# Both in-projections of a hybrid decoder layer as one list of slots, issued in program order

## The chip, the cores and the metric

The kernel runs on one core of one Trainium2 chip. The metric is the device time of one execution in microseconds (us), as the median of several runs. The core has a matrix engine (PE, with weight loads shown as PEld), a vector engine (DVE), a scalar engine (ACT), GpSimd (POOL) and a queue engine (SP). Each takes its instructions from a stream of its own, in order. DMA transfers are issued by SP, ACT and POOL, and are also taken from each of these queues in order. A DMA whose data is not ready, or whose destination is not free, holds everything that stands behind it in the same queue.

## The reference

One layer with 2048 tokens, width 1024, all in float32. A combined input projection makes 19 tiles of 128 channels, three token mixers work on them, an output projection merges them, and a squared-ReLU MLP follows.

```python
h = rmsnorm(x, norm1_g)
z = jnp.einsum("bsd,dc->bsc", h, w_in)
y_attn = attention_mixer(q, k, v)          # 6 heads, windows 128/512/2048, dilations 1/4/16
y_conv = conv_module(a, gate, ...)         # a * sigmoid(gate), causal conv of 31 taps, LayerNorm, silu
y_lru  = recurrent_mixer(gate, xr, ...)    # gelu(gate) * RG-LRU(causal conv of 4 taps)
x = x + jnp.einsum("bsc,cd->bsd", jnp.concatenate([y_attn, y_conv, y_lru], -1), w_out)
h2 = rmsnorm(x, norm2_g)
x = x + jnp.einsum("bsf,fd->bsd", jnp.square(jax.nn.relu(jnp.einsum("bsd,df->bsf", h2, w_up))), w_down)
return rmsnorm(x, final_g)
```

## The kernel before

Tokens are worked in two halves of 1024 (h = 0 and 1). Every float32 matrix is split into a rounded part and a rest, and each product is three matmuls: high by high, high by low, low by high. The split of a tile is a cast on ACT and a subtraction on DVE (`split`; `halves` does the same behind the in-projection).

The in-projection of a half makes 16 channel tiles (q and k tiles 0 to 5, conv tiles 9 to 12, recurrent tiles 13 to 18) and, apart from them, the value columns (tile -1, "V"). `COLUMN_ORDER` sets the order of the tiles; the first three of half 0 and the last two of each half are worked side by side, the others one by one. A tile takes eight steps k over the input channels. I call one step of one tile a **slot**: six matmuls of 512 columns (V: twelve of 384). There are 288 slots, 144 a half. `project` runs the steps, `load_w` loads and splits the weights of four steps, `Acts.more` loads and splits x (eight chunks of 128 channels, two loads each) and adds its squares. The sum of squares, by `norm`, becomes the factor r1 with which `evac` (and `project_v`) scales a finished tile out of PSUM on DVE. The scaled tile goes to DRAM by SP; gate tiles pass a sigmoid or gelu on ACT first. There are four main PSUM banks (two tiles), three "mix" banks and one "conv" bank.

While PE works on slots, `tick` issues pieces of half 0's mixers: attention (`attention`), then the recurrent mixer (`lru_mixer`) and the merge of the attention heads (`combine`), and as a filler the convolution on DVE (`conv_whole`, with `conv_norm` for its LayerNorm, then `conv_ahead` for half 1). In the recurrent mixer of half 0 both gates use the one conv bank: three matmuls, a sigmoid on ACT, and then three matmuls of the other gate. Half 1's mixers run later, beside the output projection and the MLP.

`out_first` loads the first operands of the output projection, `out_split` and `act_split` split them. The rows named `pair`, and `rounded` numbers 79 to 83 around the end of the in-projection, are these operands; `rounded_83` also holds the in-projection's weights.

The order of each engine's stream is made by a scheduler from priorities (`first()` and `low()` raise and lower them) and from edges written by hand: `chain` and `step` keep a mixer's instruction behind the last main instruction issued before it, and `issue_after` ties a DMA or a split to an earlier instruction. Where no edge holds, an instruction may stand elsewhere than the program wrote it.

Of the kernel before, what the change touches and what calls it, by code (L numbers as in the profile page):

```python
# [9 lines left out]
OP = mybir.AluOpType  # L10
PSUM = bass.MemoryType.PSUM

P = 128
# [66 lines left out]
def body(tc, xt, w_in, w_v, w_out, w_up, w_down, vecs, lru_wa, lru_wx, consts, g_row, out, out_rows):  # L80
# [222 lines left out]
    def project(src, group, acts, nk, evac, hook=None):  # L303
        banks = [[main_bank() if i < 2 else mix_bank() for _ in range(2)] for i in range(len(group))]
        w = {}
        if not len(acts):
            acts.between = lambda: w.update({0: load_w(src(group[0], 0))})
        for k in range(nk):
            while len(acts) < k + 1:
                acts.more()  # L310
            if hook is not None and k == hook[0]:
                hook[1]()
            for i, t in enumerate(group):
                if k % 4 == 0 and (k or i not in w):
                    w[i] = load_w(src(t, k // 4))
                products(banks[i], w[i], k % 4, acts[k], k == 0, k == nk - 1)
                tick(IN_SHARE)
            while len(acts) < (min(k + 2, nk) if k < 4 else nk):
                acts.more()
        for i, t in enumerate(group):  # L320
            evac(t, banks[i])

    last_x = [None]

    ready = set()

    def inproj(h, after):
        sq = row_tile()

        class Acts(list):  # L330
            between = None

            def more(self):
                k = len(self)
                hh, ll = slot(), slot()
                for blk in range(2):
                    cols = slice(blk * NB, (blk + 1) * NB)
                    raw = raw_tile()
                    dma = nc.sync.dma_start(raw, xt[k][:, h * HS + blk * NB:h * HS + (blk + 1) * NB])
                    if h == 0:  # L340
                        last_x[0] = dma
                    split(raw, hh[:, cols], ll[:, cols], v("norm1_g", k))
                    with tc.high_priority(offset=-20 if h == 0 and k == 0 else 0):
                        sum_squares(sq, k, blk, raw)
                    if self.between is not None:
                        self.between()
                        self.between = None
                self.append((hh, ll))

        acts = Acts()  # L350
        if h:
            while len(acts) < KT:
                acts.more()
        cols_ = groups(COLUMN_ORDER[h], h == 0, True)
        r1 = row_tile()

        def norm():
            for blk in range(2):
                cols = slice(blk * NB, (blk + 1) * NB)
                pair = [X((8 if h else 16) + i)[:, cols] for i in range(2)]  # L360
                split(sq[:, cols], *pair)
                bank = main_bank() if h else (mix_bank, conv_bank)[blk]()
                quarter_mean(bank, pair)
                nc.scalar.activation(r1[:, cols], bank, AF.Sqrt, bias=eps_r, scale=MEAN)
                nc.vector.reciprocal(r1[:, cols], r1[:, cols])

        gates = {}
        held = []
        tok = slice(h * HS, (h + 1) * HS)
        ptok = slice(32 + h * HS, 32 + (h + 1) * HS)  # L370

        def evac(t, banks):
            z = z_tile()
            ready.add((h, t))
            for b, bank in enumerate(banks):
# [3 lines left out]
                if t < CA_T:  # L379
# [10 lines left out]
                    with first():  # L390
                        if t < K_T:
                            nc.vector.scalar_tensor_tensor(zc, src, HD ** -0.5, r, op0=OP.mult, op1=OP.mult)
                        else:
                            nc.vector.tensor_mul(zc, src, r)
                else:
                    with first():
                        nc.vector.tensor_mul(zc, bank, r)
                    if CA_T <= t < CG_T:
                        nc.vector.tensor_mul(zc, zc, gates[t - CA_T][:, cols])
            if t < CA_T:  # L400
                nc.sync.dma_start(zscr[t][:, tok], z)
            elif t < CG_T:
                nc.sync.dma_start(uscr[t - CA_T][:, ptok], z)
# [9 lines left out]
        def project_v():  # L413
            if h == 0:
                nc.sync.dma_start(ident, consts[:, 6 * 256:])
            nc.sync.dma_start(rscr[tok].rearrange("(a n) -> a n", a=1), r1[0:1, :])
            rows = raw_tile()[0:8, 0:P]
            nc.sync.dma_start(rows, rscr[tok].rearrange("(c p) -> c p", p=P))
            bank = (main_bank if h else conv_bank)()
            nc.tensor.transpose(bank[:, 0:HS // P], rows, ident[0:8, 0:8])  # L420
            nc.scalar.copy(rcol[h], bank[:, :HS // P])
            for c0 in range(0, HS // P, 4):
                banks = [main_bank()[:, :VW] for _ in range(4)]
                for k in range(KT):
                    wh, wl = load_w(w_v[k])
                    ah, al = acts[k]
                    for i, bank in enumerate(banks):
# [1329 lines left out]
```

## Time and profile before

| | us |
|---|---|
| median of 3 runs | 2020.29 (2017.7 to 2020.93) |
| the profiled execution, its time | 2015.58 |
| its span, first to last instruction | 2013.4 |
| first in-projection matmul | 7.1 |
| first matmul of the output projection | 537.2 |
| PE busy in the whole span | 1947.4 (97%) |
| mean granted clock of PE | 0.989 |

A profile row of a group gives busy time, the mean of one in ns, and then the idle time that the engine had just before these instructions, with what ended it. The time around the span is 2015.58 - 2013.4 = 2.2 us. In the windows view every engine has its busy time in the stretch, with the number of instructions behind it; PEclk is the share of the full clock that PE was granted.

### The profile page before, as it was taken

How to read it: one execution, taken by the hardware profiler on the slowest of the kernel's cores; microseconds unless marked ns; L12 is line 12 of the kernel's file. 1: busy time of each engine (PE TensorE's matmuls, PEld its weight loads, DVE VectorE, ACT ScalarE, POOL GpSimd, SP SyncE). 2: the span in 40 equal slices, each digit the busy share in tenths (PEclk: the TensorE clock that was granted, in tenths of full speed). 3: DMA queues.
4: the chain of work that ended last, by engine and by line, in shares of the span. 5: the costliest groups of instructions: out<-in, count | busy, mean ns of one | idle time of the engine just before them, and what ended most of it. 6: DMA issues, size and time to landing. Idle time of an engine off the chain costs nothing.

```text
span 2013.4 us, 25522 instructions
## 1 busy us (share of the span) xinstructions
PE 1947.4 (97%) x8906; PEld 1594.7 (79%) x8906; DVE 1448.1 (72%) x1976; ACT 1046.6 (52%) x1631; POOL 203.6 (10%) x360
## 2 busy tenths in 40 slices
PE   7999987997999999999999999999999999999998
PEld 5887766786787777888888887788888888888887
DVE  7886886865477765788868899867555555576884
ACT  6145652434466765456656656546455455444353
POOL 0034200004022423000000000100000000000001
PEclk9999988999999999999999999999999999999999
DMA  5455446357556657544887687764444436786773
GB/s 170 150 175 162 132 133 210 125 196 243 184 185 188 201 149 234 190 146 157 277 278 281 234 290 251 243 199 151 148 150 154 157 141 243 249 285 217 261 262 140
DMA packets 197419, 399.77 MB, mean 199 GB/s; under 512 B 22502, under 2 KB 31094, under 8 KB 197228
## 3 DMA queue, kind: packets, MB, share of 16 engines
q1 hardware_dynamic: 173220, 328.47, 47.7%
q0 software_dynamic: 20624, 58.93, 9.7%
q10 hardware_dynamic: 3448, 10.76, 1.6%
q8 instruction: 70, 1.15, 0.2%
q14 instruction: 57, 0.47, 0.1%
HBM read 287.47 MB, written 119.00 MB: 202 GB/s over the span
## 4 chain that ended last, share of the span: by engine, by line
PE 78%; DVE 7%; DMA 6%; ACT 4%; issue 3%; POOL 1%; SPq 0%; DVEq 0%; ACTq 0%; POOLq 0%
PE bank L1169 9%; PE bank L1168 9%; PE bank L1170 9%; PE bank L1532 8%; PE bank L1531 8%; PE bank L1530 8%; PE mm L268 4%; PE mm L262 4%; PE mm L265 4%; PE bank L981 2%; PE bank L982 2%; PE bank L983 2%; DMA raw<-in_xt 2%; DVE rounded L941 1%; PE mb L726 1%
## 5 line engine op out<-in xcount | busy, mean ns | idle before, releaser
L1168 PE MATMUL bank<-rounded,pair 128*128 128x512 f32 x896 | 351.1, 392 | 1.6 <-ACT low L1177 0.9
L1169 PE MATMUL bank<-rounded,pair 128*128 128x512 f32 x896 | 351.0, 392 | 0.0
L1170 PE MATMUL bank<-rounded,pair 128*128 128x512 f32 x896 | 350.8, 391 | 0.0
L1532 PE MATMUL bank<-rounded,rounded 128*128 128x512 f32 x688 | 268.0, 389 | 1.5 <-DVE rounded L941 1.5
L1530 PE MATMUL bank<-rounded,rounded 128*128 128x512 f32 x688 | 267.8, 389 | 0.0
L1531 PE MATMUL bank<-rounded,rounded 128*128 128x512 f32 x688 | 267.7, 389 | 0.0
L941 DVE TENSOR_TENSOR rounded<-rounded 128x1024 fp32r<-128x1024 f32 (+1 forms) x172 | 186.3, 1097 | 72.6 <-ACT rounded L940 70.1
L940 ACT CAST rounded<-rounded 128x1024 fp32r<-128x1024 f32 (+1 forms) x172 | 160.5, 948 | 142.9 <-DMA rounded<-fscr 104.3
L1168 PEld LDWEIGHTS bank<-rounded,pair 128*128 128x128 f32 x896 | 168.4, 188 | 38.6 <-ACT low L1177 1.4
L1170 PEld LDWEIGHTS bank<-rounded,pair 128*128 128x128 f32 x896 | 168.2, 188 | 35.9 <-issue 0.2
L262 PE MATMUL mm<-rounded,rounded 128*128 128x512 f32 x496 | 163.3, 407 | 34.4 <-ACT rounded L242 21.7
L1169 PEld LDWEIGHTS bank<-rounded,pair 128*128 128x128 f32 x896 | 168.3, 188 | 35.4 <-issue 0.2
L265 PE MATMUL mm<-rounded,rounded 128*128 128x512 f32 x496 | 162.5, 403 | 0.0
L268 PE MATMUL mm<-rounded,rounded 128*128 128x512 f32 x496 | 159.6, 402 | 2.0 <-DVE rounded L243 2.0
L1532 PEld LDWEIGHTS bank<-rounded,rounded 128*128 128x128 f32 x688 | 129.1, 188 | 29.0 <-DVE rounded L941 2.3
L1530 PEld LDWEIGHTS bank<-rounded,rounded 128*128 128x128 f32 x688 | 129.2, 188 | 27.2 <-DVE u L1540 0.2
L1531 PEld LDWEIGHTS bank<-rounded,rounded 128*128 128x128 f32 x688 | 129.1, 188 | 26.9
L940 ACT CAST rounded<-kept 128x1024 fp32r<-128x1024 f32 x80 | 84.1, 1051 | 123.4 <-DVE kept L1340 56.7
L262 PEld LDWEIGHTS mm<-rounded,rounded 128*128 128x128 f32 x496 | 94.4, 195 | 56.4 <-ACT rounded L242 25.0
L242 ACT CAST rounded<-raw 128x512 fp32r<-128x512 f32 (+1 forms) x96 | 54.9, 582 | 143.7 <-PE mm L265 86.0
L940 ACT CAST pair<-wraw 128x1024 fp32r<-128x1024 f32 x64 | 67.1, 1048 | 113.5 <-PE bank L1169 109.3
L941 DVE TENSOR_TENSOR pair<-wraw,pair 128x1024 fp32r<-128x1024 f32 x64 | 78.2, 1222 | 61.5 <-ACT pair L940 61.5
(370 smaller groups left out, 3709.7 us busy)
## 6 DMA issues: line engine op xcount, KB each, us to landing
fscr<-low SPq DMA_DIRECT2D x224, 256.0 KB, 2.2
rounded<-fscr SPq DMA_DIRECT2D x112, 512.0 KB, 3.8
second<-in_w_down SPq DMA_DIRECT2D x80, 512.0 KB, 5.4
kept<-in_w_down SPq DMA_DIRECT2D x48, 512.0 KB, 4.9
raw<-in_w_in SPq DMA_DIRECT2D x64, 256.0 KB, 3.6
low<-in_w_up SPq DMA_DIRECT2D x64, 256.0 KB, 3.2
wraw<-in_w_up SPq DMA_DIRECT2D x64, 256.0 KB, 3.0
raw<-in_xt SPq DMA_DIRECT2D x32, 256.0 KB, 3.8
```

What stands on the lines that cost most here:

```text
L242: nc.scalar.copy(h, raw)
L262: nc.tensor.matmul(bank, wh[:, sl], ah[:, cols], start=first_, stop=False)
L265: nc.tensor.matmul(bank, wh[:, sl], al[:, cols], start=False, stop=False)
L268: nc.tensor.matmul(bank, wl[:, sl], ah[:, cols], start=False, stop=last_)
L940: nc.scalar.copy(h, raw)
L941: nc.vector.tensor_sub(l, raw, f32(h))
L1168: nc.tensor.matmul(bank, wh[:, sl], hi(x), start=fresh and k == 0, stop=False, **kw)
L1169: nc.tensor.matmul(bank, wh[:, sl], lo(x), start=False, stop=False, **kw)
L1170: nc.tensor.matmul(bank, wl[:, sl], hi(x), start=False, stop=k == KH - 1, **kw)
L1530: nc.tensor.matmul(banks[j], th[:, c], sh[:, x], start=fresh and k0, stop=False, **kw)
L1531: nc.tensor.matmul(banks[j], th[:, c], sl[:, x], start=False, stop=False, **kw)
L1532: nc.tensor.matmul(banks[j], tl[:, c], sh[:, x], start=False, stop=k1, **kw)
```

## The change

`inproj`, `project` and `norm` go. `in_projections` writes both halves as one list of 288 slots. For each slot it is fixed at which earlier slot a weight unit is split (four slots ahead of its use, two for V) and at which slot its load is issued (that many plus two slots earlier again), with at most five loads outstanding. The sixteen loads of x for half 1, which stood together, are spread from 40 slots before the turn (slot 144, where half 1 begins) to five slots behind it. x of half 0 is loaded in whole 1024-token chunks into other buffers and split one chunk per three slots. The two norms are generators (`means`) that advance by one piece a slot. `evac` stands right behind a tile's last slot. The DMAs of the norm's row move from SP to POOL, and so does the load of `ident`.

The whole is issued inside `manual_schedule` for all five engines, and the hand-made edges are left out there (`in_order`). The splits of the output projection's first operands (`out_ready`) are issued behind the last slot, and the loads of these operands eight slots before the end of the list instead of sixteen. The matmuls ahead of the output projection are the same in number.

```diff
+    def in_projections(hooks):
+        slots, units, begin = [], [], []
+        for h in range(2):
+            begin.append(len(slots))
+            for grp in groups(COLUMN_ORDER[h], h == 0, True):
+                for c0 in (0, 4) if grp[0] < 0 else (0,):
+                    now = {}
+                    for k in range(KT):
+                        for t in grp:
+                            if t < 0 or k % 4 == 0:
...
+                                units.append(dict(src=src, first=len(slots), lead=2 if t < 0 else 7 if len(slots) == 3 * KT else 4))
+                                now[t] = units[-1]
+                            now[t]["last"] = len(slots)
+                            slots.append((h, grp, c0, k, t, now[t]))
+        turn = begin[1]
+        todo, at = [], 0
+        for n, u in enumerate(units):
+            at = max(at, u["first"] - u["lead"], units[n - 4]["last"] + 1 if n >= 4 else 0)
...
+            todo.append([at, len(todo), at - u["lead"] - 2, load, consume])
...
+        for k in range(KT):
+            for blk in range(2):
+                i = 2 * k + blk
+                at = turn + (4 * i - 40 if k < 4 else 2 * i - 24 if k < 6 else (0, 2, 3, 5)[i - 12])
...
+                todo.append([at, len(todo), at - 6, load, consume])
+        todo.sort(key=lambda x: x[:2])
+        loaded = []
+
+        def pump(s, most=5):
+            while todo and len(loaded) < most and todo[0][2] <= s:
+                x = todo.pop(0)
+                loaded.append((x[0], x[4], x[3]()))
...
+        def means(h):
...
+            for blk in range(2):
+                cols = slice(blk * NB, (blk + 1) * NB)
+                bank = mix_bank()
+                quarter_mean(bank, pairs[blk])
                 nc.scalar.activation(r1[:, cols], bank, AF.Sqrt, bias=eps_r, scale=MEAN)
+            yield
+            for blk in range(2):
+                cols = slice(blk * NB, (blk + 1) * NB)
                 nc.vector.reciprocal(r1[:, cols], r1[:, cols])
+                yield
...
+        norms = {15 + begin[0]: means(0), 7 + turn: means(1)}
+        norm, banks, late = None, {}, []
+        for s, (h, grp, c0, k, t, unit) in enumerate(slots):
+            norm = norms.get(s, norm)
+            if norm is not None:
+                next(norm, None)
+            if s < 14 and (s == 0 or s % 2):
+                x_whole((s + 1) // 2)
+            while loaded and loaded[0][0] <= s:
+                consume_next()
+                pump(s)
+            pump(s)
+            hooks(s, begin, len(slots), h, grp, k, t)
...
+            elif k == KT - 1 and h and s < turn + KT:
+                late.append((h, t, banks[t]))
+            elif k == KT - 1 and t == grp[-1]:
+                for i in grp:
+                    evac(h, i, banks[i])
+            if late and s == turn + 12:
+                evac(*late.pop())
+            tick(IN_SHARE * (1.5 if t < 0 else 1.0))
...
-            if i.engine in held_engines and i.engine in mains:
+            if i.engine in held_engines and i.engine in mains and not in_order[0]:
...
-        last_act = next(i for i in reversed(nc.cur_bb.bb.instructions) if i.engine == mybir.EngineType.Activation)
-        with tc.issue_after(last_act):
-            out_split(0, pairs)
-            for n in range(KT):
-                act_split(1, n)
+
+    def out_ready(pairs):
+        out_split(0, pairs)
+        for n in range(KT):
+            act_split(1, n)
...
-    inproj(1, between)
+    engines = mybir.EngineType
+    in_order[0] = True
+    with tc.manual_schedule(engines={engines.PE, engines.DVE, engines.Activation, engines.SP, engines.Pool}):
+        in_projections(hooks)
+        out_ready(pairs)
+    in_order[0] = False
```

What it does to the streams is seen at three places. The first is SP's queue at the turn between the halves. `raw<-in_xt` are the loads of x for half 1, `raw<-in_w_in` the weight loads. Before:

```order
L339 DMA raw_101<-in_xt 128x512
L339 DMA raw_102<-in_xt 128x512
L339 DMA raw_103<-in_xt 128x512
L339 DMA raw_99<-in_xt 128x512
L411 DMA lscr<-z 128x1024
L251 DMA raw_100<-in_w_in 128x512
L409 DMA gscr<-z 128x1024
L251 DMA raw_101<-in_w_in 128x512
L251 DMA raw_102<-in_w_in 128x512
```

The same place now:

```order
L371 DMA raw_99<-in_xt 128x512
L331 DMA raw_100<-in_w_in 128x512
L371 DMA raw_101<-in_xt 128x512
L371 DMA raw_102<-in_xt 128x512
L371 DMA raw_103<-in_xt 128x512
L331 DMA raw_99<-in_w_in 128x512
L462 DMA lscr<-z 128x1024
L460 DMA gscr<-z 128x1024
L371 DMA raw_100<-in_xt 128x512
L331 DMA raw_101<-in_w_in 128x512
```

The loads of x and of weights now alternate, and the weights of half 1 no longer stand behind all of its x.

The second place is PE in the recurrent mixer: `cb<-mr` are its two gates in the one conv bank, the `mm` rows are slots. Before:

```order
L268 MATMUL mm<-rounded_78,rounded_83 128x512 x2
L576 MATMUL cb<-mr 128x512
L577 MATMUL cb<-mr 128x512
L578 MATMUL cb<-mr 128x512
L576 MATMUL cb<-mr 128x512
L577 MATMUL cb<-mr 128x512
L578 MATMUL cb<-mr 128x512
L262 MATMUL mm<-rounded_81,rounded_83 128x512 x2
L265 MATMUL mm<-rounded_81,rounded_83 128x512
L576 MATMUL cb<-mr 128x512
L577 MATMUL cb<-mr 128x512
L578 MATMUL cb<-mr 128x512
```

And now:

```order
L268 MATMUL mm<-rounded_82,rounded_83 128x512 x2
L634 MATMUL cb<-mr 128x512
L635 MATMUL cb<-mr 128x512
L636 MATMUL cb<-mr 128x512
L634 MATMUL cb<-mr 128x512
L635 MATMUL cb<-mr 128x512
L636 MATMUL cb<-mr 128x512
L262 MATMUL mm<-rounded_82,rounded_83 128x512 x2
L265 MATMUL mm<-rounded_82,rounded_83 128x512 x2
```

Before, most second gates stood some matmuls of a slot behind the first; now all six pairs stand together, and the last pair comes ahead of V, where before three of the twelve triples stood within V.

The third place is ACT at the end of the in-projection. `raw` casts are weights, `z<-z` the gelu of the last tile, `pair` and `rounded_79` to `rounded_83` the operands of the output projection. Its first matmul takes `rounded_79` and `pair_3855` before the change, `rounded_79` and `pair_3891` after it. Before:

```order
L242 CAST rounded_83<-raw_103 128x512
L408 ACT_TABLE_LOAD
L408 ACTIVATE z<-z 128x1024
L940 CAST pair_3855<-pair_3856 128x1024
L940 CAST rounded_79<-rounded_79 128x512 x4
L940 CAST rounded_80<-rounded_80 128x512 x4
L940 CAST rounded_81<-rounded_81 128x512 x4
L940 CAST rounded_82<-rounded_82 128x512
L940 CAST rounded_83<-rounded_83 128x1024
L940 CAST rounded_82<-rounded_82 128x512 x3
L408 ACTIVATE z<-z 128x1024
```

And now:

```order
L242 CAST rounded_83<-raw_100 128x512
L998 CAST rounded_81<-rounded_81 128x512 x2
L998 CAST pair_3893<-pair_3894 128x1024
L998 CAST rounded_83<-rounded_83 128x1024
L998 CAST rounded_81<-rounded_81 128x512 x2
L998 CAST rounded_82<-rounded_82 128x512 x2
L459 ACTIVATE z<-z 128x1024
L998 CAST pair_3891<-pair_3892 128x1024
L998 CAST rounded_79<-rounded_79 128x512 x4
L998 CAST rounded_80<-rounded_80 128x512 x4
```

The casts that the first output matmul needs stood ahead of the last gelu and now stand behind it, and operands that are needed later (`rounded_81`, `rounded_82`, part of `rounded_83`) stand ahead of them.

More of the change, by code (lines that the diff above doesn't have):

```diff
@@ L301, in groups @@
         return out_
[L303 to L321, printed above, removed]
@@ L345, in more @@
[L345 to L357, printed above, removed]
+                    sum_squares(sq, k, blk, raw)
+                todo.append([at, len(todo), at - 6, load, consume])
+        todo.sort(key=lambda x: x[:2])
@@ L358, in norm, with consume_next @@
+        loaded = []
[3 more added lines that the diff above has]
+                loaded.append((x[0], x[4], x[3]()))
+        def consume_next():
+            at, do, raw = loaded.pop(0)
+            do(raw)
+        def means(h):
+            pairs = []
             for blk in range(2):
                 cols = slice(blk * NB, (blk + 1) * NB)
-                pair = [X((8 if h else 16) + i)[:, cols] for i in range(2)]
@@ L361, in norm @@
-                split(sq[:, cols], *pair)
-                bank = main_bank() if h else (mix_bank, conv_bank)[blk]()
-                quarter_mean(bank, pair)
+                pairs.append([X((8 if h else 16) + i)[:, cols] for i in range(2)])
+                split(sq[:, cols], *pairs[-1])
+            for _ in range(3):
+                yield
[3 more added lines that the diff above has]
+                quarter_mean(bank, pairs[blk])
@@ L367, in inproj, with evac @@
+            for _ in range(6):
+                yield
+            bank = mix_bank()
+            nc.tensor.transpose(bank[:, 0:HS // P], rows, ident[0:8, 0:8])
+            nc.scalar.copy(rcol[h], bank[:, :HS // P])
+            yield
         gates = {}
[L368 to L372, printed above, removed]
+        def evac(h, t, banks):
+            ready.add((h, t))
             z = z_tile()
-            ready.add((h, t))
+            tok = slice(h * HS, (h + 1) * HS)
+            ptok = slice(32 + h * HS, 32 + (h + 1) * HS)
@@ L389, in evac @@
                         r = r.rearrange("p (s r) -> p s r", r=16)
[L390 to L394, printed above, removed]
-                else:
[L396 to L399, printed above, removed]
+                    if t < K_T:
+                        nc.vector.scalar_tensor_tensor(zc, src, HD ** -0.5, r, op0=OP.mult, op1=OP.mult)
+                    else:
+                        nc.vector.tensor_mul(zc, src, r)
+                else:
+                    nc.vector.tensor_mul(zc, bank, r)
             if t < CA_T:
```

156 lines of the change are left out of this document (85 added, 71 removed).

## The prediction

> **What bounds the kernel now.** I read the page's first part first: PE is busy for 97% of the span, so a change can only win back PE's idle time and its time at a low clock. Then I cut the in-projection, which ends with the first output matmul at 537.2 us, into stretches (the windows view; the first column after the length is PE's busy time, then PEld, DVE, ACT, POOL, PEclk, DMA share, GB/s):
>
> ```profile
> span 2013.4 us, 25522 instructions
> PE 1947.4 (97%) x8906; PEld 1594.7 (79%) x8906; DVE 1448.1 (72%) x1976; ACT 1046.6 (52%) x1631; POOL 203.6 (10%) x360
> ...
> 7.10:46.80 39.70, 36.50 (x148) 28.55 (x148) 34.07 (x60) 28.11 (x47) 0.00 (x0) 1.00 0.60 184
> 46.80:114.90 68.10, 67.19 (x337) 60.16 (x338) 59.40 (x75) 15.30 (x27) 7.19 (x12) 1.00 0.48 155
> 114.90:225.20 110.30, 108.69 (x610) 84.63 (x609) 77.40 (x182) 61.62 (x165) 43.69 (x72) 1.00 0.57 162
> 225.20:268.20 43.00, 37.14 (x181) 29.52 (x179) 41.58 (x67) 29.47 (x61) 3.06 (x5) 0.99 0.49 153
> 268.20:310.30 42.10, 39.87 (x154) 31.69 (x155) 30.95 (x38) 19.43 (x27) 1.62 (x3) 0.89 0.40 135
> 310.30:332.90 22.60, 11.80 (x52) 9.22 (x50) 12.41 (x14) 6.34 (x7) 0.85 (x2) 0.83 0.23 78
> 332.90:387.00 54.10, 51.07 (x205) 40.74 (x206) 42.74 (x45) 18.88 (x25) 3.47 (x7) 0.91 0.48 170
> 387.00:449.80 62.80, 60.46 (x258) 48.63 (x256) 45.03 (x50) 24.97 (x30) 5.33 (x10) 0.97 0.58 197
> 449.80:500.10 50.30, 37.30 (x202) 34.66 (x202) 27.04 (x50) 20.88 (x32) 17.74 (x33) 0.96 0.73 241
> 500.10:537.20 37.10, 35.85 (x145) 29.03 (x145) 20.05 (x31) 14.86 (x24) 7.75 (x14) 0.92 0.60 186
> ```
>
> PE's idle time is length less busy time; what the clock takes is length times (1 - PEclk). **A**, 7.1 to 225.2 (the first half's tiles up to the end of attention, slots 0 to 119): 3.2 + 0.9 + 1.6 = 5.7 us idle. **B**, 225.2 to 310.3 (around the turn, slots 120 to 167): 5.9 + 2.2 = 8.1 idle and 0.4 + 4.6 = 5.0 of clock. **C**, 310.3 to 537.2: 10.8 + 3.0 + 2.3 + 13.0 + 1.2 = 30.3 idle and 3.8 + 4.9 + 1.9 + 2.0 + 3.0 = 15.6 of clock. That is some 65 us on the table; the matmuls ahead of 537.2 stay the same, and so does the work behind. Who ended PE's waits says the waits view (total, times, longest):
>
> ```profile
> PE mm L262 <- ACT rounded L242: 21.7, 3, 9.3
> PE mm L262 <- DVE z L438: 7.6, 1, 7.6
> ...
> PE cb L576 <- ACT wide L579: 1.8, 2, 1.0
> ```
>
> Weights that were split late (L242), three times for 21.7 us, are just what fixed places address.
>
> **A, worth +2.** Fixed places can take 4 of the 5.7 us. But both row means now take a mix bank while the third tile holds two of three, so the second waits for a square root on ACT with its table load: 1.28 + 0.69 us by the rows below (L518), some 2 us. Sum +2, between -2 (the `setup` splits now wait in order for their loads) and +4.
>
> **B, worth 0.** Here I count DVE's instructions between slots 120 and 168 in the new order. Durations:
>
> ```profile
> L246 DVE SCALAR_TENSOR_TENSOR rounded<-raw,vec,rounded 128x512 fp32r<-128x512 f32 x32 | 23.8, 746 | 3.8 <-ACT rounded L245 3.8
> L277 DVE TENSOR_TENSOR row<-row,tmp 128x512 f32<-128x512 f32 x28 | 19.1, 684 | 0.0
> L397 DVE TENSOR_TENSOR z<-mm,row 128x512 f32<-128x512 f32 x38 | 24.3, 681 | 39.1 <-PE mm L268 38.8
> L365 DVE RECIPROCAL row<-row 128x512 f32<-128x512 f32 x4 | 13.1, 3309 | 1.4 <-ACT row L364 1.4
> L519 DVE RECIPROCAL wide<-wide 128x512 f32<-128x512 f32 x2 | 6.7, 3352 | 2.2 <-ACT wide L518 2.2
> ...
> 342.07 1.28 DVE L486 SCALAR_TENSOR_TENSOR wide<-wide,vec 128x1024 f32<-128x1024 f32 x1
> 343.27 0.69 DVE L243 TENSOR_TENSOR rounded<-raw,rounded 128x512 fp32r<-128x512 f32 x1
> ```
>
> The last two rows show that a tap of 1.28 us lets the next instruction start after 1.20, so I take 0.08 off each. 20 taps x 1.20 = 24.0; 18 splits x 0.61 = 11.0; 11 splits of x at 0.67 and 11 sums at 0.60 = 14.0; 12 evacuations and 12 small operations of the LayerNorm at 0.60 = 14.4; four reciprocals, 13.0; a gate product and the end of attention, 2. Sum 78.4 us, against 85.1 - 8.1 - 5.0 = 72.0 of PE. DVE is the bound there before and after (41.58 of 43.00 us busy in the row 225.20). Five of the sixteen splits of x move ahead of it, but in order DVE stands while ACT does the root ahead of each pair of reciprocals (2.2 and 1.4 us in the rows) and the casts of DVE's own sums: some 7 us, which makes 85. Worth 0; from +12 (PE sets the pace) to -5 (twice the waits).
>
> **C, worth +25.** Of 46 us some waits come back. First the gates of the recurrent mixer (six pairs, one bank). Rows of two such neighbours:
>
> ```profile
> 323.69 1.28 ACT L518 ACT_TABLE_LOAD   x1 [11.01 <-PE cb L283]
> 324.99 0.69 ACT L518 ACTIVATE wide<-cb,eps_l 128x512 f32<-128x512 f32 x1
> ...
> 361.28 0.40 PE L578 MATMUL cb<-mr 128*128 128x512 f32 x1
> 361.72 0.69 ACT L579 ACTIVATE wide<-cb,vec 128x512 f32<-128x512 f32 x1 [15.03 <-PE cb L578]
> 362.46 0.50 PE L576 MATMUL cb<-mr 128*128 128x512 f32 x1 [0.78 <-ACT wide L579]
> ```
>
> Each pair stops PE for 0.8 to 1.0 us (the last row, and the longest of L576 in the waits view), and the first pair of each of three tiles for a table load of 1.28 more, since that load starts only when PE is done: 6 x 0.9 + 3 x 1.28 = 9. [...]
>
> Second, DVE in order behind ACT's exponentials and roots:
>
> ```profile
> L581 DVE TENSOR_TENSOR wide<-wide 128x1024 f32<-128x1024 f32 x3 | 3.6, 1215 | 2.9 <-ACT wide L579 2.9
> L592 DVE TENSOR_TENSOR wide<-wide 128x1024 f32<-128x1024 f32 x3 | 3.7, 1219 | 0.8 <-ACT wide L590 0.8
> L585 ACT ACT_TABLE_LOAD x3 | 3.8, 1283 | 0.1
> L590 ACT ACT_TABLE_LOAD x3 | 3.8, 1283 | 0.1
> L585 ACT ACTIVATE wide<-wide,splus 128x1024 f32<-128x1024 f32 x3 | 3.5, 1153 | 0.0
> L588 ACT ACTIVATE wide<-wide 128x1024 f32<-128x1024 f32 x3 | 3.2, 1056 | 1.3 <-DVE wide L581 1.3
> L590 ACT ACTIVATE wide<-wide 128x1024 f32<-128x1024 f32 x3 | 3.2, 1061 | 1.4 <-DVE wide L589 1.4
> ```
>
> At least 2.9 + 0.8 = 4 us as now; at most the whole ACT chain of three tiles, 3.8 + 3.8 + 3.5 twice (exponential, tanh) + 3.2 + 3.2 = 21. I take 8, nearer the low end, since two to four slots (a slot is six matmuls at 0.227, 1.36 us) lie between the pieces and weights are split four slots ahead. Third, V runs beside the merge of the heads, where DMA moved 241 GB/s (row 449.80) and the longest wait of that stretch (7.6) arose; loads now have a fixed lead of four slots, the output operands no longer stand among them, and I leave 4 us, from 0 to 10. 46 - 9 - 8 - 4 = 25, from 6 (9 + 21 + 10 stay) to 37 (5 + 4 stay, no load late).
>
> **D, the handover, worth -9.** Before, the casts for the output projection ran under the last tile, and PE waited 1.25 us:
>
> ```profile
> 528.65 1.05 ACT L940 CAST rounded<-rounded 128x1024 fp32r<-128x1024 f32 x1 [1.46 <-DMA rounded<-out_w]
> 530.64 1.66 ACT L940 CAST rounded<-rounded 128x512 fp32r<-128x512 f32 x3 [0.93 <-DMA rounded<-mscr]
> 537.05 1.06 ACT L408 ACTIVATE z<-z 128x1024 f32<-128x1024 f32 x1 [4.75 <-DVE z L397]
> 537.16 0.47 PE L981 MATMUL bank<-rounded,pair 128*128 128x512 f32 x1 [1.25 <-DVE z L397]
> ...
> 267.30:274.10 6.80, 5.68 (x13) 3.96 (x14) 6.61 (x11) 3.73 (x7) 0.00 (x0) 0.50 0.81 237
> 496.00:506.30 10.30, 6.20 (x15) 4.79 (x16) 5.73 (x9) 2.72 (x4) 5.77 (x10) 0.50 0.79 262
> ```
>
> Now ACT has ahead of the needed casts those of `rounded_82`, whose load is the eleventh of eleven 256 to 768 KB operand loads and a 512 KB store. The first overwrites x of step 0, so it can go 14 slots before the end, 19 us. 6.3 MB at the 241 GB/s of row 449.80 take 26 us. They land 7 us after the last slot; at a third more speed, right behind it. Behind that stand a cast (0.55), the gelu (1.06), the cast of `pair_3891` (1.05) and one of `rounded_79` (0.55): 3.2 us. I take about the middle, 3 + 3.2 = 6.2 idle, 5 more than now. A stop of that size costs clock: the half-clock stretch after the stop before 268.2 lasted 6.8 us, which at full load is 3.4 us; so -5 - 3.4, about -9. Bounds: -2 (all landed, only ACT's order is left) and -20 (a stop of 12, with the 10.3 us of half clock of the last row and the loads of half 1's attention beside them). [...]
>
> **Sum.** 2 + 0 + 25 - 9 = 18 us. The profiled execution took 2015.58 us (2013.4 of span and 2.2 around), so 1998 in its measure; the median of the runs shown is 2020.29, 4.7 above it, and 18 less is 2002.
>
> **Rivals.** *PE sets the pace everywhere*: DVE has room in C (row 387.00: 45.03 busy of 62.80), so only the gates' 9 us stay, the loads land in time, and A and B give 4 and 6: 4 + 6 + 37 - 2 = 45, time 1975. Against it stands B, where DVE's 78 us exceed PE's 72. *DVE and ACT set the pace* (the other side): in order DVE stands at each root, exponential and sigmoid, and PE behind its weights. The price is the low end of B, C and D's estimate: 2 - 5 + 6 - 9 = -6, and -9 with three more table loads of the LayerNorm exposed; time 2026 to 2029. It decides from the point at which ACT's results come later than the four slots (5.4 us) by which weights lead. For it: ACT needs 1.28 + 1.15 + 1.15 + 1.06 us in a row between two pieces; against it: today's idle rows for the same places are 0.8 to 2.9 us for three tiles. *The handover eats it*: operands land late enough for the low end of D, and half of C's gates and waits more come back: 2 + 0 + 20 - 20 = 2, time 2018.
>
> **Chances.** Forecast 0.50, PE's pace 0.20, DVE and ACT 0.18, handover 0.12. A measurement of this kernel can tell 0.2%, 4 us. Forecast and first rival are faster: 0.70; the last is within it, 0.12; slower 0.18. The range 1976 to 2028 reaches from 44 us gained to 8 lost; the forecast's own is 1985 to 2015.
>
> **What would show it.** The first output matmul should come near 519 us (537.2 - 18), after a stop of about 6 us that ACT's operand casts end, with PEclk at 0.5 behind it. The waits of `mm` for L242 should be under 5 us in all. The gate rows should show six stops of about 1 to 2 us. If DVE is busy through slots 120 to 168 and that stretch takes 85 us again, B holds; if it takes under 78, I overcounted. I am wrong if the stretch behind the turn is no shorter than now, or if the stop at the handover exceeds 12 us.

## The result and the profile after

The changed kernel takes 2078.18 us (median), the kernel before on the same chip 2018.99: a ratio of 1.0291, 95% interval 1.0267 to 1.0316. It is 59 us slower, where 18 faster was forecast. The spans of the two profiled executions, 2078.5 and 2013.4 us, are 65 us apart. The first output matmul comes at 595.7 us instead of 537.2, so 58.5 us are lost inside the in-projection and some 7 behind it (2078.5 - 595.7 against 2013.4 - 537.2).

The windows view of both kernels, cut at the same slots (0, 40, 64, 120, 168, 240, and the first output matmul; columns as in the prediction). Before:

```profile
7.10:70.40 63.30, 59.20 (x245) 46.38 (x246) 49.27 (x82) 33.12 (x53) 0.00 (x0) 1.00 0.54 169
70.40:114.90 44.50, 44.50 (x242) 42.34 (x241) 44.21 (x53) 10.28 (x20) 7.19 (x12) 1.00 0.51 160
114.90:225.20 110.30, 108.69 (x610) 84.63 (x609) 77.40 (x182) 61.62 (x165) 43.69 (x72) 1.00 0.57 162
225.20:310.30 85.10, 77.02 (x334) 61.20 (x333) 72.53 (x104) 48.89 (x88) 4.67 (x8) 0.94 0.45 144
310.30:438.20 127.90, 111.74 (x461) 89.28 (x460) 98.21 (x104) 44.09 (x55) 9.66 (x18) 0.92 0.45 154
438.20:537.20 99.00, 84.74 (x398) 73.00 (x396) 49.07 (x83) 41.84 (x61) 25.49 (x46) 0.95 0.70 229
```

After:

```profile
7.30:87.10 79.80, 64.16 (x245) 49.44 (x246) 47.99 (x73) 32.16 (x41) 2.42 (x6) 0.89 0.35 120
87.10:132.60 45.50, 44.58 (x241) 42.23 (x241) 43.50 (x53) 11.11 (x21) 7.16 (x12) 1.00 0.55 161
132.60:273.10 140.50, 117.72 (x614) 90.76 (x613) 78.56 (x186) 62.67 (x176) 43.70 (x72) 0.96 0.47 134
273.10:383.60 110.50, 85.94 (x333) 65.04 (x333) 82.88 (x104) 48.62 (x82) 6.13 (x11) 0.86 0.30 95
383.60:510.00 126.40, 115.06 (x470) 90.38 (x469) 99.91 (x102) 46.82 (x59) 5.50 (x11) 0.95 0.52 173
510.00:595.70 85.70, 78.50 (x386) 68.88 (x384) 38.26 (x71) 25.21 (x40) 28.91 (x53) 0.99 0.82 266
```

Three stretches lost: slots 0 to 39 (16.5 us), the attention in slots 64 to 119 (30.2) and the turn in slots 120 to 167 (25.4). Behind the turn 1.5 and 13.3 us were gained. PE's idle time (length less busy time) rose from 44 to 82 us, and what the clock took (length times one less PEclk) from 20 to 37. So the loss is 38 us of waits that the kernel before did not have, and 17 us more of slow clock. PE's waits (total, times, longest) name three kinds:

```profile
PE mb L813 <- DVE stat L815: 20.0, 24, 1.8
PE mm L262 <- ACT rounded L242: 15.3, 3, 7.3
PE cb L282 <- ACT wr L242: 12.7, 3, 9.5
PE mm L262 <- DVE z L449: 7.0, 1, 7.0
PE cb L635 <- DVE mr L243: 4.7, 3, 2.4
PE cb L634 <- ACT wide L637: 4.7, 6, 0.8
PE bank L1039 <- ACT rounded L998: 4.6, 1, 4.6
```

The first row is the attention. A unit's scores are two halves of one bank (L813); after each, DVE reads the half (L815). In program order the second half's matmuls stand right behind the first's and wait for that read. PE's rows after, and DVE's of the same time:

```profile
170.90 0.40 PE L813 MATMUL mb<-mr 128*128 128x256 f32 x2
173.11 0.51 PE L813 MATMUL mb<-mr 128*128 128x256 f32 x2 [1.80 <-DVE stat L815]
```

```profile
170.87 1.92 DVE L447 TENSOR_TENSOR z<-mm,row 128x512 f32<-128x512 f32 x2 [2.39 <-PE mm L268]
172.64 0.40 DVE L815 CUSTOM_DVE_ANT_0 m<-mb,m 128x256 f32<-128x256 f32 x1
```

DVE is at an evacuation, and PE stands for it. In the kernel before the scheduler had put in-projection matmuls between two such halves (L755 there), and nothing waits here; its waits of this kind come to 1.1 us in the whole attention:

```profile
136.66 0.40 PE L755 MATMUL mb<-mr 128*128 128x256 f32 x2
136.89 0.63 PE L262 MATMUL mm<-rounded,rounded 128*128 128x512 f32 x2
...
137.82 0.39 PE L268 MATMUL mm<-rounded,rounded 128*128 128x512 f32 x1
138.05 0.40 PE L755 MATMUL mb<-mr 128*128 128x256 f32 x2
```

The start shows two more, in ACT's rows after. The square of an x chunk is written in place (L361), so it waits for DVE's subtraction, and the next chunk's cast (L245) stands behind it: 3.55 us from one square to the next (the next starts at 23.07). And `setup`, now in its written place, holds ACT for the two small weights' transfers, with the in-projection's weight casts behind them:

```profile
19.52 1.06 ACT L361 ACTIVATE wide<-wide 128x1024 f32<-128x1024 f32 x1 [1.44 <-DVE rounded L246]
20.48 1.14 ACT L245 ACTIVATE rounded<-wide,vec 128x1024 fp32r<-128x1024 f32 x1
...
60.22 0.51 ACT L242 CAST rounded<-wide 128x384 fp32r<-128x384 f32 x1 [3.86 <-DMA wide<-in_lru_wa]
67.14 0.51 ACT L242 CAST rounded<-wide 128x384 fp32r<-128x384 f32 x1 [6.41 <-DMA wide<-in_lru_wx]
```

At the turn it is DVE's order. Its rows:

```profile
319.24 2.48 DVE L544 SCALAR_TENSOR_TENSOR wide<-wide,vec 128x1024 f32<-128x1024 f32 x2
322.89 2.49 DVE L449 TENSOR_TENSOR z<-mm,row 128x512 f32<-128x512 f32 x4
344.16 3.35 DVE L577 RECIPROCAL wide<-wide 128x512 f32<-128x512 f32 x1 [1.07 <-ACT wide L576]
351.83 6.57 DVE L409 RECIPROCAL row<-row 128x512 f32<-128x512 f32 x2 [2.99 <-ACT row L405]
361.76 0.69 DVE L243 TENSOR_TENSOR wr<-wide,wr 128x512 fp32r<-128x512 f32 x1 [1.03 <-ACT wr L242]
```

Convolution taps (L544) and splits of x stand ahead of an evacuation (L449) for which PE waits 7.0 us; then both norms' reciprocals stand ahead of the convolution norm's split, for which PE waits 9.5.

### The profile page after: what moved, and what is told of

It is laid out like the page before. It is cut to its first block, busy times and chain, and to the rows that moved or that the text cites. A ratio compares the mean times of both kernels' runs of the same rounds, so it can differ in the third digit from the quotient of the medians.

```text
span 2078.5 us, 25402 instructions
## 1 busy us (share of the span) xinstructions
PE 1970.0 (95%) x8906; PEld 1604.6 (77%) x8906; DVE 1454.3 (70%) x1958; ACT 1036.6 (50%) x1612; POOL 205.7 (10%) x365
## 4 chain that ended last, share of the span: by engine, by line
PE 65%; issue 5%; DVE 5%; DMA 4%; ACT 3%; POOL 0%; SPq 0%; ACTq 0%; DVEq 0%; POOLq 0%
PE bank L1227 10%; PE bank L1226 10%; PE bank L1228 9%; PE bank L1588 7%; PE bank L1590 7%; PE bank L1589 7%; PE bank L1039 3%; PE bank L1040 3%; PE bank L1041 3%; DVE rounded L999 1%; DMA rounded<-out_w 1%; DMA second<-in_w_down 1%; PE cb L813 1%; DMA rounded<-fscr 1%; PE mb L784 1%
## 5 line engine op out<-in xcount | busy, mean ns | idle before, releaser
L262 PE MATMUL mm<-rounded,rounded 128*128 128x512 f32 x496 | 166.9, 419 | 23.2 <-ACT rounded L242 15.3
L1588 PEld LDWEIGHTS bank<-rounded,rounded 128*128 128x128 f32 x688 | 129.1, 188 | 27.6 <-DVE u L1598 0.4
L262 PEld LDWEIGHTS mm<-rounded,rounded 128*128 128x128 f32 x496 | 95.3, 199 | 45.8 <-ACT rounded L242 16.7
L999 DVE TENSOR_TENSOR rounded<-kept,rounded 128x1024 fp32r<-128x1024 f32 x80 | 97.9, 1223 | 33.4 <-ACT rounded L998 32.9
```

The costliest lines, as they stand in the source:

```text
L262: nc.tensor.matmul(bank, wh[:, sl], ah[:, cols], start=first_, stop=False)
L999: nc.vector.tensor_sub(l, raw, f32(h))
L1588: nc.tensor.matmul(banks[j], th[:, c], sh[:, x], start=fresh and k0, stop=False, **kw)
```

## The experiments

Each kernel's time, its ratio to the kernel before on the same chip, and the time of six stretches of slots in its profiled execution (from the start times of the slots' first matmuls; the last column is the first output matmul).

| kernel | median us | ratio (95%) | 0-39 | 40-63 | 64-119 | 120-167 | 168-239 | 240-287 | first output |
|---|---|---|---|---|---|---|---|---|---|
| before | 2018.99 | | 63.3 | 44.5 | 110.3 | 85.1 | 127.8 | 99.0 | 537.2 |
| changed | 2078.18 | 1.0291 (1.0267-1.0316) | 79.8 | 45.5 | 140.5 | 110.4 | 126.4 | 85.7 | 595.7 |
| halves | 2060.65 | 1.0216 (1.0199-1.0233) | 80.8 | 45.5 | 126.8 | 105.0 | 122.1 | 86.0 | 573.4 |
| setup | 2065.36 | 1.0237 (1.0221-1.0252) | 68.2 | 45.9 | 139.6 | 107.9 | 123.7 | 84.6 | 577.4 |
| xsq | 2069.70 | 1.0260 (1.0234-1.0287) | 75.3 | 45.5 | 141.0 | 107.8 | 123.7 | 86.1 | 586.6 |
| turn | 2078.61 | 1.0290 (1.0264-1.0316) | 82.0 | 45.5 | 140.9 | 87.7 | 120.3 | 111.0 | 594.8 |
| pefree | 2056.25 | 1.0195 (1.0177-1.0213) | 78.7 | 44.4 | 122.8 | 101.1 | 126.0 | 88.8 | 569.1 |
| free | 2008.25 | 0.9952 (0.9936-0.9968) | 72.8 | 54.3 | 118.1 | 80.4 | 111.9 | 84.5 | 532.4 |
| late | 2000.01 | 0.9913 (0.9890-0.9936) | 58.6 | 44.5 | 117.1 | 79.1 | 123.6 | 84.8 | 514.7 |
| tuned1 | 2035.53 | 1.0089 (1.0074-1.0104) | 62.4 | 46.0 | 129.2 | 98.7 | 115.0 | 95.1 | 553.6 |
| tuned2 | 2036.31 | 1.0091 (1.0070-1.0112) | 64.3 | 45.8 | 128.8 | 88.1 | 116.8 | 98.0 | 549.1 |
| late240 | 2025.24 | 1.0035 (1.0024-1.0046) | 59.1 | 44.4 | 119.6 | 79.4 | 131.5 | 100.9 | 542.0 |
| late280 | 2029.79 | 1.0056 (1.0040-1.0073) | 59.1 | 44.4 | 118.2 | 80.3 | 131.6 | 102.6 | 543.2 |
| late280b | 2040.38 | 1.0115 (1.0098-1.0132) | 58.8 | 44.4 | 115.1 | 104.5 | 119.4 | 106.1 | 555.6 |
| lategate | 2005.27 | 0.9933 (0.9914-0.9953) | 58.7 | 44.4 | 120.8 | 79.1 | 116.8 | 94.4 | 521.4 |
| latefirst | 2003.74 | 0.9936 (0.9921-0.9951) | 58.8 | 44.5 | 117.7 | 72.6 | 132.6 | 87.9 | 521.4 |
| late2 | 1991.92 | 0.9864 (0.9844-0.9883) | 59.0 | 44.4 | 118.5 | 80.4 | 115.1 | 83.3 | 508.1 |

### The suspected causes, one at a time

**halves**

```diff
@@ attention
                         1.0, -3.0e38, OP.add, OP.max, top[:, j:j + 1])
+                    if j == 0 and h == 0:
+                        yield HALF        # resumed inside the next slot
@@ products
             nc.tensor.matmul(bank, wh[:, sl], al[:, cols], start=False, stop=False)
+        between()                         # here: the second half
```

> The changed kernel (2078 us), with the two halves of an attention unit's scores (L813) set apart: the second half is issued behind the first four matmuls of the next slot instead of right behind the first half. Theory 1, the order inside the attention: TensorE stands at the second half until VectorE has read the first one (24 waits, 20.0 us) and four slow-clock stretches follow; both go, slots 64 to 119 fall from 140 us to 112 to 120, and the time to 2050 to 2058. Rival, VectorE is the bound there: the same 20 us turn up as waits of TensorE for evacuations (mm for L449 and L447) and the time stays above 2070.

Slots 64 to 119 won back 13.7 of their 30 us. They took 126.8 us and the kernel 2060.7, both above the ranges of theory 1. The evacuations did not take the waits over, so the rival is out. The wait for L815 (L819 here) fell from 20.0 us to 4.3; what is left waits for the splits of the next keys (L715):

```profile
PE mb L817 <- DVE mr L715: 5.1, 6, 1.4
PE cb L638 <- ACT wide L641: 4.7, 6, 0.8
...
PE mb L817 <- DVE stat L819: 4.3, 9, 0.9
```

**setup**

```diff
+        elif s == 2 * KT - 2:
+            gate_loads()      # the lru weights' transfers, slot 14
         elif s == 3 * KT + 2:
             setup()           # their splits and stores only
@@
+        softplus()
         in_projections(hooks)
```

> The changed kernel with the set-up taken out of the way: the lru weight loads issued at slot 14 instead of 26, and the twenty small softplus operations put ahead of the slots. Theory 1: the gaps of 6.35 us (at 69.9) and 3.14 us (at 75.1) and most of the 13.7 us of half clock behind them go; slots 24 to 39 fall from 35.1 us to 24 to 26, the time to 2060 to 2066. Rival, the slots wait there for weights and evacuations whatever the set-up does: under 4 us, 2074 or more.

Slots 24 to 39 took 22.1 us instead of 35.0, and the time against the kernel before fell by 11 us. Theory 1 holds.

**xsq**

```diff
                 x_whole((s + 1) // 2)
+                if s:
+                    x_square((s - 1) // 2)
```

> The changed kernel with the square of an x chunk put behind the split of the next one. Theory 1: the ring split, subtract, square in place, split (3.55 us for each chunk in the rows of ScalarE and VectorE) opens to VectorE's 2.5 us a chunk; slots 8 to 23 fall from 31.9 us to 25 to 27, the time to 2070 to 2073. Rival, the loads of whole chunks set the pace: 2076 to 2080.

Slots 8 to 23 took 25.1 us instead of 31.9. Theory 1 holds: ACT's square no longer stands for DVE in its rows. Of the 16.5 us that slots 0 to 39 had lost, `setup` accounts for 11.6 and the square for 4.5.

```profile
16.13 1.14 ACT L245 ACTIVATE rounded<-wide,vec 128x1024 fp32r<-128x1024 f32 x1
17.18 1.04 ACT L364 ACTIVATE wide<-wide 128x1024 f32<-128x1024 f32 x1
```

**turn**

```diff
+            paused[0] = turn - 8 <= s < turn + 8
@@ tick
-        credit[0] -= cost or step(filler)
+        credit[0] -= cost or (0 if paused[0] else step(filler))
```

> The changed kernel with the convolution held back for 16 slots about the turn (slots 136 to 151), so that it comes after the second half's mean squares instead of among the x splits. Theory 1, the chain of VectorE and ScalarE in order at the turn: the gaps of 7.02 us (323.7) and 9.52 us (361.8) and their slow clock go, slots 120 to 167 fall from 110 us to 88 to 95, the time to 2055 to 2065. Rival, VectorE's work is only moved: the gates and the merge behind it, 16 slots later, give it back in slots 168 to 279, 2072 to 2084.

Both theories are right in their place. The turn fell from 110.4 to 87.7 us; the rival's sum is what counts, since slots 240 to 287 rose by 25. The gates came 15 slots later and the merge 11, beside V and the loads of the output projection's operands, and the handover stood 14.1 us:

```profile
PE bank L1041 <- ACT rounded L1000: 14.1, 1, 14.1
PE cb L636 <- ACT wide L639: 6.4, 4, 4.1
```

### Order or list

**pefree** gives PE alone back to the scheduler:

```diff
-    with tc.manual_schedule(engines={engines.PE, engines.DVE, engines.Activation, engines.SP, engines.Pool}):
+    with tc.manual_schedule(engines={engines.DVE, engines.Activation, engines.SP, engines.Pool}):
```

> The changed kernel with TensorE alone given back to the scheduler; VectorE, ScalarE and both DMA-issuing queues stay in program order. Theory 1a, TensorE's own order costs most of it: slots 64 to 119 come to 112 to 122 us, the time to 2040 to 2055. Theory 1b, TensorE waits because VectorE and ScalarE are held in order: the attention stays within 8 us of 140, the turn at 75 to 80, the time at 2065 to 2080.

The attention came to 122.8 us, and the time to 2056, both within 2 us of theory 1a's ranges: PE's own order made 18 of its 30. The start (78.7) and most of the turn (101.1) stayed, so those come from the order of the others; there PE waits for evacuations (`PE mm L262 <- DVE z L449`, 23.6 us in three).

**free** leaves out `manual_schedule` and sets `in_order` nowhere; **late** does so up to slot 167:

```diff
+            if s == turn + 24:
+                in_order[0] = True
+                manual.enter_context(tc.manual_schedule(engines={E.PE, E.DVE, E.Activation, E.SP, E.Pool}))
```

> The changed kernel's list of slots, loads, norms and mixer steps, but with the scheduler that set the order in the kernel before back on all five queues (the work itself, its tiles, banks and transfers stay as changed). Theory 1, the order of issue costs the time: the waits of TensorE inside the attention and at the turn go, and the time comes to 2005 to 2030. Rival, what the list itself changed (whole x chunks with their square in place, the set-up's place, the gates' multiply, six queued loads) costs it: above 2050.

> The changed kernel with program order on the five queues only from slot 168 on (behind the turn), and the scheduler ahead of it. Theory A, the order gains 15 us in slots 168 to 287 by itself: the first part as before or near it (303 to 312 us to slot 168), the rest 212 us, the time 1998 to 2010. Theory B, those 15 us are only work that the slots ahead had done already: the rest takes 222 to 232 us again, the time 2012 to 2030.

With the same list, loads, banks and pieces, the scheduler (with its hand-made edges back) takes 2008 us, as theory 1 said: program order as written costs 70 us, and the list gains 10 against the kernel before. Behind slot 168 free takes 196.5 us up to the first output matmul, the least of all kernels here, where the changed one takes 212.1. In free the first matmul comes at 10.3 us and slots 0 to 63 take 127 us. Its DMA rows for the first 70 us show 3.15 MB on ACT's queue, which late does not have there: nothing held the two late weights back any more. The run late280 below holds these loads and leaves all but the last eight slots to the scheduler, and its slots 0 to 63 take 103.5 us: the slow start goes with the early loads.

```profile
q10 hardware_dynamic: 592, 3.15, 14.0%
```

Late keeps the start (58.6 us) and takes 208 us behind slot 168, where the kernel before takes 227. It is faster than both kernels, and theory A holds.

### All in order, tuned

**tuned1** takes the edits of halves, setup and xsq, holds the convolution over slots 138 to 147, puts the merge (`combine`) ahead of the gates, fetches the next gate's input early, gives the second gate another bank, and leaves more slots between a split and its matmuls in the gates (one more) and in the LayerNorm (three instead of one). Part of it:

```diff
-                        bank = mix_bank() if h and m else conv_bank()
+                        bank = mix_bank() if m else conv_bank()
@@
             yield from attention(0)
+            yield from combine(0)
             yield from until(0, "conv", *range(LG_T, LX_T + 3))
             yield from lru_mixer(0)
-            yield from combine(0)
```

> All five queues in program order, with the causes taken out together: score halves apart, set-up early, the x square behind the next split, the merge ahead of the gates and the convolution held for ten slots at the turn, three slots instead of one between a normalisation's split and its matmuls, the second gate in another bank, the next gate's input fetched early. If the parts add (18 + 13 + 8 us as measured, 15 to 22 at the turn, 5 to 8 at the gates): 2009 to 2025. Rival, VectorE is the bound from slot 64 to 240 and takes back what the turn and the gates free: 2035 to 2042.

It came out at the rival's time. The first three edits alone had won 16, 11 and 7 us against the kernel before, 34 of the 41 that tuned1 won; of the 20 to 30 expected of the other edits 7 came. In part that had a plain cause: ACT's rows show the merge's exponential standing 12.26 us for a subtraction on DVE (L933) of values that the merge loads just ahead of it (from `sscr`), weights' casts behind it.

```profile
267.24 1.28 ACT L934 ACT_TABLE_LOAD   x1
280.78 0.24 ACT L934 ACTIVATE m<-m 128x48 f32<-128x48 f32 x1 [12.26 <-DVE m L933]
280.93 0.60 ACT L250 CAST rounded<-raw 128x512 fp32r<-128x512 f32 x1
```

**tuned2** puts that exponential twelve slots further behind its loads:

```diff
-        yield 0
-        yield 0
-        yield 0
+        for _ in range(3 if h else 15):
+            yield 0
```

> All five queues in program order with the same seven edits as before, and the merge's first operation on ScalarE put twelve slots further behind its loads. Theory A, the 12.3 us for which ScalarE stood at the merge's exponential (weights queued behind it, TensorE waiting 7.6 us, slow clock behind) are a fixed place too near to a DMA: slots 120 to 135 fall from 36.8 us to 26 to 29, the time to 2023 to 2029. Theory B, VectorE's backlog at the turn takes it back: above 2031.

Slots 120 to 135 fell from 36.8 to 27.7 us, as theory A said, but the median did not follow. 1.8 and 2.9 us came back behind the turn, and the 4.5 us by which the first output matmul is earlier are no more than the runs differ by. I did not find a program order of the whole in-projection that beats the scheduler.

### What gained behind the turn

**late240** and **late280** move the switch to program order to slots 240 and 280. With the scheduler in charge there, I held the late weights as in the kernel before, and so changed two things at once:

```diff
-            if s == turn + 24:
+            if s == turn + 96:      # late280: len(slots) - KT
@@
-            nc.scalar.dma_start(out_w[2 * i:2 * i + 2], w_out[2 * i:2 * i + 2])
+            with tc.issue_after(next(i for i in reversed(nc.cur_bb.bb.instructions) if i.engine == mybir.EngineType.Activation)):
+                nc.scalar.dma_start(out_w[2 * i:2 * i + 2], w_out[2 * i:2 * i + 2])
```

> The scheduler up to slot 240, program order on the five queues from there to the handover; the late loads of the two weights on ScalarE's queue held back as in the kernel before. Theory A, program order costs time in slots 200 to 239 as well (73 us there under order from slot 168, 63 us under the scheduler alone): those slots fall to 62 to 65 us and the time to 1986 to 1994. Theory B, the scheduler has to give those 10 us back behind slot 240, where VectorE's work is then later: 1996 to 2004.

> The same with program order only in the last eight slots and the handover: does order gain anything at all. Theory A, nothing but the handover: within 5 us of order from slot 240. Theory B, order saves time in the V slots (240 to 279), which the scheduler alone does in 72 us and order in 69 to 70: 3 to 8 us slower than order from slot 240.

Both theories of late240 fell: 2025 us. Slots 168 to 287 took 232 and 234 us, 24 to 26 more than in late. The late280 run came 4.6 us behind late240, which both of its theories allow. In both the scheduler put gate matmuls into PE's stream ahead of a split that came late; late240's waits, two of the three at slots 183 and 215:

```profile
PE cb L639 <- ACT mr L242: 17.9, 3, 11.5
```

**late280b** changes the hold alone (`issue_after` an instruction of slot 120):

> The scheduler up to the last eight slots, as in the run with order only there, but the loads of the two late weights freed from slot 120 on instead of one behind the other from slot 176. Theory A, what held those loads back on ScalarE's queue is what made the scheduler slow behind the turn (131.6 us for slots 168 to 239 with it, 112 us without): those slots fall to 112 to 118 us and the time to 1985 to 2005. Theory B, the scheduler's order is simply another from kernel to kernel (gates placed where TensorE stands for them): 125 to 135 us again, 2015 to 2035.

At 2040 us neither theory gave the time. Slots 168 to 239 did fall, from 131.6 to 119.4 us, near theory A's 112 to 118, so the hold changed what the scheduler did there; but the turn took 104.5 us instead of 80.3, and slots 240 to 287 took 106.1. With another hold the scheduler was slow elsewhere. The slots in which the twelve matmul groups of the gates stand go with the time of slots 240 to 287, which has V in slots 248 to 263:

| kernel | slots of the gates | slots 240-287, us |
|---|---|---|
| before | 179, 191, 191, 192, 210 to 214, 239, 249, 249, 249 | 99.0 |
| free | 179 to 184, 203 to 207, 226 to 231 | 84.5 |
| late (and changed) | 179 to 183, 202 to 206, 226 to 230 | 84.8 (85.7) |
| late240 | 183 to 199, 215 to 231, 244 to 247 | 100.9 |
| late280b | 187 to 219, 234 to 238, 247 to 249 | 106.1 |

Where the scheduler puts gates right ahead of V or among its slots, the stretch takes 99 to 106 us; where they end by slot 231, 84 to 86 (88 in latefirst). One wait goes with it: at slot 264, the first behind V, PE waits for V's evacuation on DVE, 7.6 us before, 6.9 in late280 and 9.7 in late280b, but 2.3 in free and none in late (late240 stands 8.7 us at slots 244 to 248 instead). That the gates' place is the cause is not shown: no run moved them alone, and lategate, below, takes 94.4 us with its gates ended by slot 237. Program order pins the gates; why the scheduler left them early only in free stays open.

**lategate** is late with one slot more between a gate's split and its matmuls, and the second gate in another bank; **late2** also fetches the next gate's input one tile ahead, which brings the merge forward again:

```diff
+                if h == 0 and t < 2:
+                    ahead = fetch(t0, t + 1)      # x and gate weights of the next tile
```

> Program order from slot 168, with one slot more between the split of a gate's input and the gate's matmuls and the second gate's matmuls in another bank. Theory A, the ten waits at the gates (7 us) and the slow clock behind them are what order costs in slots 200 to 239: they fall from 73 us to 62 to 67, the time to 1990 to 1995. Theory B, VectorE is the bound there (63 us of work in 73): under 3 us, 1997 to 2003.

> Program order from slot 168 with the gates eased (one slot more, second bank), and the next gate input fetched one tile ahead, so that the merge of the heads comes back to the slots it had (two earlier, even). Theory A, the V slots lost 10 us in the run with eased gates because the merge came five slots later beside V's own splits: slots 240 to 287 fall from 94 us to 84 to 88, slots 168 to 239 stay at 115 to 119, the time 1993 to 1998. Theory B, VectorE has the same work and gives it back wherever it is moved: 2000 to 2006.

In lategate slots 168 to 239 gained 6.8 us and slots 240 to 287 lost 9.6, and at 2005 us both of its theories missed. Its merge began at slot 248, where late has it at 244. In late2 the merge begins at slot 240, and both stretches are short, 115.1 and 83.3. Theory A of late2 holds, and late2 is the fastest kernel here: 0.9864 of the time before, interval 0.9844 to 0.9883.

**latefirst** is late with the evacuations' priority put back (`with first():` around L445 to L449):

> Program order from slot 168, and ahead of it the scheduler with the priority for evacuations that the kernel before had and the change dropped. Theory A, the dropped priority is what keeps slots 64 to 119 at 117 us where the kernel before has 110: they fall to 108 to 112, the time to 1992 to 1996. Theory B, the 7.9 us of waits there come from the new places of the x and weight splits ahead of the scores: 115 to 120 again, 1997 to 2004.

The attention stayed at 117.7 us, as theory B said, so the priority is not what it lacks against the 110.3 before. The turn gained 6.5 us and slots 168 to 239 lost 9. What the 7 us in the attention come from stays open; late's waits there are again mostly those of the second score half (L820 there is L815):

```profile
PE mb L818 <- DVE stat L820: 4.3, 4, 1.8
```

## Why the prediction was wrong

**A (+2; measured -48, of which attention -30).** This is the step that failed most. "Fixed places can take 4 of the 5.7 us" looked at the waits that the trace had, and not at those that the scheduler had hidden. The one wait that it added, the second row mean behind a square root, came as forecast: 2.1 us for 2. But the order makes three kinds that it did not count or kept too small: score halves with nothing between them, `setup` on a transfer (bounded at -2; put out of the way it gave 11), and the in-place square (not counted; 7). Setting the score halves apart gave back 14 of the attention's 30 us, and leaving slots 0 to 167 to the scheduler (late) gave 23; the other 7 stay open.

**B (0; measured -25).** The work was counted well: 78.4 us forecast for DVE, 82.9 busy. The term for standing was mis-sized: some 7 us for DVE in order behind ACT, where it stood 110.5 - 82.9 = 27.6. The turn run bears it out in part: with the convolution out of the way the stretch takes 87.7, of which DVE is busy 69.8, so it stands 18 us; the other 13 us gained are work that moved behind the stretch. What failed is the sum as such: adding busy times and a few known waits came out as a floor. At 351.83 DVE had stood 2.99 us for ACT, its reciprocals took another 6.57, and PE stood 9.5 us until 361.78.

**C (+25, less 5 for the stop of D that lies in it, so +20; measured +14.8).** Sign and size held, the reasons only in part. Late weights did go: the longest wait of `mm` for L242 left in C is 0.8 us. But of the 21.7 us that the prediction named for them only 9.3 lay in C; 5.3 lay at the turn, and 7.1 were the very first weights, for which PE still waits 7.3. The gates' 9 us were 9.4, but otherwise made. The six stops behind the sigmoid are 0.8 us each (4.7), and the table load added nothing in the rows below: ACT loads the table (439.95) while PE still waits for DVE's split. That the load starts only when PE is done was a misreading; in the kernel before, too, one load (393.37) ran ahead, and its sigmoid then waited 0.98 us for the matmuls (395.64). The rest is DVE's split, late behind evacuations and taps (L635, 4.7):

```profile
439.87 1.90 DVE L445 SCALAR_TENSOR_TENSOR z<-mm,row 128x512 f32<-128x512 f32 x2
441.62 0.68 DVE L243 TENSOR_TENSOR mr<-wide,mr 128x512 fp32r<-128x512 f32 x1
...
439.95 1.28 ACT L637 ACT_TABLE_LOAD   x1
443.61 0.69 ACT L637 ACTIVATE wide<-cb,vec 128x512 f32<-128x512 f32 x1 [2.37 <-PE cb L636]
```

Nor is order the only way to such a gain: free, where the scheduler set the order, did the same slots in 196.5 us.

**D (stop of 6.2 us and slow clock; measured 4.6 and 6.8 us at half clock).** Right, and by the cause named: ACT's operand casts wait for the loads.

```profile
588.37 1.05 ACT L998 CAST rounded<-rounded 128x1024 fp32r<-128x1024 f32 x1 [5.72 <-DMA rounded<-out_w]
...
595.68 1.22 PE L1039 MATMUL bank<-rounded,pair 128*128 128x512 f32 x2 [4.56 <-ACT rounded L998]
```

```profile
594.70:601.50 6.80, 5.82 (x13) 4.18 (x14) 6.80 (x12) 6.55 (x12) 0.00 (x0) 0.50 0.57 193
```

**The rivals.** "DVE and ACT set the pace" had the sign and the mechanism (PE behind engines that stand in order), but with the low ends of B, C and D for its price it came to 6 to 9 us lost instead of 59, and it looked behind the turn, where the order did well. Its chance, 0.18, was too low because A's range ended at -2: no rival asked what the order does where the scheduler had no idle time.

**The signs named ahead.** First output matmul near 519: it came at 595.7. Waits for L242 under 5 us in all: 15.3, 7.3 of it at the very start and 6.4 by `setup`. Gate stops of 1 to 2 us: 0.8, with two of 2.0 and 2.4 from DVE. Turn of 85 us: 110.5. Handover of 6: 4.6.

## What to carry to other kernels

Before a scheduler's order is replaced by program order, look for what it hides: wherever two dependent instructions of one engine stand next to each other in the code with another engine's answer between them, something independent has to be written between them, even in stretches that show no idle time today (PE's waits between the score halves rose from 1.1 to 20.0 us). Give every step that reads a transfer or a DRAM round trip its distance in slots: in the changed kernel ACT stood 3.86 and 6.41 us for the two transfers of `setup` with the weights' casts behind it, and PE 6.35. And order can be taken where it pays only: here the scheduler ahead of slot 168 and fixed places behind it (late2, 0.986 of the time before) beat both whole solutions that were tried (free 0.995, tuned1 1.009).

## What the runs showed of the hardware

In the changed kernel short stops went with a lower granted clock. Rows of its windows view, with the granted clock as the third number from the end:

```profile
34.90:38.30 3.40, 3.40 (x9) 2.64 (x8) 1.80 (x2) 1.50 (x2) 0.00 (x0) 0.50 0.00 0
65.60:79.30 13.70, 6.26 (x14) 4.48 (x15) 9.11 (x35) 3.81 (x8) 0.00 (x0) 0.50 0.30 86
150.90:157.70 6.80, 5.73 (x25) 4.39 (x25) 2.71 (x7) 1.57 (x5) 0.00 (x0) 0.50 0.52 161
215.80:219.20 3.40, 3.40 (x12) 2.36 (x13) 1.78 (x4) 1.42 (x6) 0.00 (x0) 0.50 0.96 318
```

These four half-clock stretches last 3.4, 13.7, 6.8 and 3.4 us. In the first, two matmuls of 512 columns start 0.85 us behind the two before (34.91 and 35.76), after it 0.47 (39.24 and 39.71). The third begins with the second of two stops, 1.33 and 1.12 us within 3.3 us; the fourth comes right behind stops of 1.32, 0.28 and 1.26 us. The single stops of 2.12 us at 43.36 and of 1.80 us at 173.11 have none behind them: 43.36 to 52 and 173.11 to 185 were granted 1.00. So 2.5 us of short waits, close together, went with 6.8 us at half clock; half of that, 3.4 us, is my estimate of what it cost at full load.
